# Weight sums by adding transfers that read DRAM, and six raw places as three pairs

## The chip, the cores and the metric

The kernel runs on one core of a Trainium2 chip. The metric is the device time of one execution in microseconds (us): the median of three runs before the change is 1502.31 us (1502.04 to 1503.32). A profile of one further execution shows what each engine did in it. The engines are TensorE (PE, with its weight loads PEld), VectorE (DVE), ScalarE (ACT), GpSimd (POOL) and SyncE (SP), and 16 DMA engines move data.

## The reference, cut to what matters

The layer normalises, mixes tokens in three branches, and then runs an MLP. The change lies in the MLP, on 256 tokens, with D_MODEL 2048 and D_FF 8192, all float32:

```python
x = x + _rms_norm(mix, norm_mix_post[l])
hdn = jnp.square(jax.nn.relu(_rms_norm(x, norm_mlp_pre[l]) @ w_mlp_up[l]))
x = x + _rms_norm(hdn @ w_mlp_down[l], norm_mlp_post[l])
```

## The kernel before

All big weights lie in DRAM as one stream `wst` of pieces of 128 x 1024 float32 (512 KB), in the order of use. A piece goes from DRAM to a raw tile by a DMA that SP issues (line 162 in `wraw`, three places under the tag "raw"), and is then split into two parts of type float32r for TensorE: ScalarE copies it to `whi` with rounding (line 173), and VectorE subtracts that from the raw tile to get the rest, `wlo` (line 175). Each matmul is then done with the high part and, over half the columns or as a third product, the low one.

The mixing part, up to some 830 us, and the last stretch, from some 1441 us, use this stream alone, with an order that is partly written out by hand (`manual_schedule`). Between them lies the stretch that the change touches. It interleaves two kinds of work:

- *up products* (`up`, lines 1370 to 1383): 64 hidden column blocks, each in two halves, each half with one piece of the up weights from the stream (`wraw`, line 162) and 16 matmuls in `gemm` (lines 191, 195, 197). `hidden` (lines 1348 to 1368) then makes the squared relu of the sum and `forms` (lines 1385 to 1397) the seven combinations of four parts of the hidden tensor that the next kind needs.
- *down products* (`down`, lines 1399 to 1475): for most of the hidden rows the product with `w_mlp_down` is done in Winograd's form of a two by two block product, with seven multiplications for eight. There are 28 blocks: four groups of 3, 4, 4 and 3 (`SIZES`) by two column halves `sb`. A block has four weight quarters, called "22", "12", "11" and "21", each 128 x 1024 in SBUF.

The seven products of a block need the quarters and running sums of them. `prep(f, d)` makes the operand of product `f` (line 1408). For f = 3 it loads 22 and 12 (`braw`, DMA at line 1331), splits 22, and VectorE adds 12 to 22 (line 1411). For f = 7 it loads 11, splits 22, VectorE adds 11 to 22, and a DMA that GpSimd issues adds 11 to 12 (`dma_add`, line 1414, with `accum_op` add, from tile to tile). For f = 1 it splits 11. For f = 6 it loads 21, splits 22, and a DMA adds 21 to 22. f = 2 splits 21, f = 5 splits 12 and f = 4 splits 22. `run(f, d, hl)` issues the six matmuls of a product (lines 1434 to 1436), and `post` adds finished sums to the output tiles (line 1441).

A block of the list (lines 1541 to 1554) is: product 3, an up half, product 4 of the block before, then products 7 and 1, an up half, 6 and 2, an up half, 5, an up half. The eight blocks in `THREE` (numbers 18, 20, 21 and 23 to 27, counted from 0) have three up halves instead of four. `drive` (line 1301) prepares an item one ahead of the item that runs. The order of instructions on each engine is not written out in this stretch: the framework's planner makes it from the order in the program and from its own costs, and it puts in the waits.

The raw tiles of the quarters share one tag, "raw2", with six places. A place is free for the next load once everything that reads or writes the tile in it is done: the splits, VectorE's sums, and the adding transfer that reads it as a source or writes it as a target. SP issues loads of both tags in one queue, so a load that waits for its place holds every load behind it.

A quarter in DRAM is two runs of 512 columns in each of 128 rows of two neighbouring pieces of the stream (`second` gives the number of the first), so a load by `braw` has 256 runs of 2 KB; a load at line 162 has 128 runs of 4 KB. The adding transfer before reads 128 rows of 4 KB of one tile and adds them to 128 rows of another.

At the end, the split parts of the last three pieces of the stream get places of their own from tag "raw2" (`spare`, line 1567).

Of the kernel before, what the change touches and what calls it, by code (L numbers as in the profile page):

```python
# [11 lines left out]
F32 = mybir.dt.float32  # L12
F32R = mybir.dt.float32r
AF = mybir.ActivationFunctionType
ALU = mybir.AluOpType
# [8 lines left out]
HALF = 1024  # L24
# [28 lines left out]
def hybrid_block(ctx, tc, xt, x, gains, params, consts, lora, gup, wst, out):  # L53
    nc = tc.nc
    V, A, G, PE = nc.vector, nc.scalar, nc.gpsimd, nc.tensor
# [10 lines left out]
    def nm(s):  # L66
        uid[0] += 1
        return f"{s}_{uid[0]}"

    def gps():  # L70
        return pg.tile([128, 512], F32, tag="gps", name=nm("gps"), bufs=4)

    def mps():
        return pm.tile([128, 512], F32, tag="mps", name=nm("mps"), bufs=4)
# [207 lines left out]
    def g1(w=T):  # L282
        return rp.tile([128, T], F32, tag="g1", name=nm("g1"), bufs=21)
# [772 lines left out]
    for hf in range(2):  # L1056
        for s, mo in (("k", MU_K), ("r", MU_R), ("v", MU_V)):
            for p in range(4 * hf, 4 * hf + 4):
                ps = unit(upk)
                d = g1()  # L1060
# [99 lines left out]
    for c in range(0, D, 512):  # L1160
        for tt in range(2):
            loads.append(lambda tt=tt, c=c: nc.sync.dma_start(out=x1[tt][:, c:c + 512],
                                                              in_=x[tt * 128:tt * 128 + 128, c:c + 512]))
# [3 lines left out]
    def junk():  # L1167
        return p2.tile([128, 512], F32, tag="junk", name=nm("junk"), bufs=2)
# [153 lines left out]
    def second(g, cg):  # L1322

        return base + 64 * (g // 4) + 32 + 8 * cg + 2 * (g % 4)

    def braw(c0, d, n):

        i, j = int(n[0]) - 1, int(n[1]) - 1
        u = second(d, c0 // 512 + j)
        raw = p3.tile([128, HALF], F32, tag="raw2", name=nm("raw"), bufs=6)  # L1330
        nc.sync.dma_start(out=raw.rearrange("p (r c) -> p r c", r=2),
                          in_=wst[u:u + 2, :, 512 * i:512 * i + 512].rearrange("r p c -> p r c"))
        return raw

    def parts(raw):
        wsplit(raw)
        return wq.pop()
# [61 lines left out]
    def down(q, sb):  # L1399

        d0 = sum(SIZES[:q])
        dn = d0 + SIZES[q] - 1
        Q, R, vx = {}, {}, {}
        c0 = 1024 * sb
        y11, y12 = ys[0][:, c0:c0 + 512], ys[0][:, c0 + 512:c0 + 1024]
        y21, y22 = ys[1][:, c0:c0 + 512], ys[1][:, c0 + 512:c0 + 1024]

        def prep(f, d):

            def add(a, b):  # L1410
                V.tensor_tensor(R[d, a], R[d, a], R[d, b], ALU.add)  # L1411

            def dma_add(a, b):
                G.dma_start(out=R[d, a], in_=R[d, b], accum_op=ALU.add)  # L1414

            for n in {3: ("22", "12"), 7: ("11",), 6: ("21",)}.get(f, ()):
                R[d, n] = braw(c0, d, n)
            r = parts(R[d, {1: "11", 2: "21", 5: "12"}.get(f, "22")])
            if f == 3:
                add("22", "12")  # L1420
            elif f == 7:
                add("22", "11")
                dma_add("12", "11")
            elif f == 6:
                dma_add("22", "21")
            return r

        def run(f, d, hl):
            if d == d0:
                Q[f] = gps() if f in (3, 7, 1) else mps()  # L1430
            for i in range(2):
                a, b = fmh[2 * d + i][:, AF_[f], :], fml[2 * d + i][:, AF_[f], :]
                w, wl = (x[:, 512 * i:512 * i + 512] for x in hl)
                PE.matmul(Q[f], a, w, start=d == d0 and i == 0, stop=False)  # L1434
                PE.matmul(Q[f], b, w, start=False, stop=False)  # L1435
                PE.matmul(Q[f], a, wl, start=False, stop=d == dn and i == 1)  # L1436
            if d == dn:
                post(f)

        def acc(y, p, op=ALU.add):  # L1440
            sums.append(lambda: V.tensor_tensor(y, y, p, op))

        def first(y, p, op=ALU.add):

            if q == 0:
                sums.append(lambda: A.activation(y, p, AF.Copy, scale=1.0 if op == ALU.add else -1.0))
            else:
                acc(y, p, op)

        def post(f):  # L1450

            if f == 3:
                first(y12, Q[3], ALU.subtract)
            elif f == 1:
                first(y11, Q[1])
            elif f == 6:
                v = vx["v"] = junk()
                posts.append(lambda: A.activation(v, Q[6], AF.Copy))
                acc(v, Q[1], ALU.subtract)
                acc(y12, v)  # L1460
                acc(v, Q[7], ALU.subtract)
                first(y22, v)
            elif f == 2:
                acc(y11, Q[2])
            elif f == 5:
                acc(y12, Q[5], ALU.subtract)
                acc(y22, Q[5], ALU.subtract)
            elif f == 4:
                first(y21, Q[4])
                acc(y21, vx["v"], ALU.subtract)  # L1470

        def item(f, d):
            return (lambda: prep(f, d), lambda hl: run(f, d, hl), 0)

        return [{f: item(f, d) for f in range(1, 8)} for d in range(d0, dn + 1)]

    po.close()
    p3 = ctx.enter_context(tc.tile_pool(name="p3", bufs=1))
# [88 lines left out]
    def spare(n):  # L1567

        if n < wst.shape[0] - 3:
            return None  # L1570
        return [p3.tile([128, HALF], F32, tag="raw2", name=nm("kw"), bufs=6).bitcast(F32R) for _ in range(2)]

    home[0] = spare
    for g in range(4):
        gs = slice(512 * g, 512 * g + 512)
        for tt, ps in enumerate(tok(hp, 4 if g == 3 else 1)):
# [8 lines left out]
            if g == 3:  # L1585
                for c, w in (0, 512), (512, 512), (1024, 512), (1536, 256), (1792, 256):
# [3 lines left out]
                        out=out[tt * 128:tt * 128 + 128, cs], in_=x1[tt][:, cs])  # L1590
# [125 lines left out]
```

## Time and profile before

| | |
|---|---|
| median of three runs | 1502.31 us |
| the profiled execution | 1503.08 us, its span 1501.2 us |
| DMA, whole span | 312.19 MB, mean 208 GB/s; from HBM 279.24 MB |
| adding transfers | 56, of 512 KB each |
| loads of quarters | 112, of 512 KB each |
| loads by line 162 | 398, of 512 KB each |

How to read the rows that follow: a time in front of a row of the timeline or of the chain of waits is its start in us from the start of the span. `raw<-in_wst_dram` is a load, `raw<-raw` an adding transfer, q1 the queue of SP's transfers and q0 that of GpSimd's. SPq is SP's queue. In a row of waits stand the total in us, the count and the longest. In a row of groups stand, behind the bar, the busy time, the mean of one in ns, and the idle time before them with what ended it. For a transfer, the last number of its row is the median us from issue to landing. The line numbers are those of the kernel before.

### The profile page before, as it was taken

The numbers are of one execution on the slowest core, as the hardware profiler recorded it, in microseconds if no ns is written. First come the engines' busy times: TensorE is split into PE (matmuls) and PEld (weight loads), VectorE is DVE, ScalarE is ACT, GpSimd is POOL, SyncE is SP. The second block draws the span as 40 slices with busy tenths as digits, with TensorE's granted clock in tenths as the row PEclk, the third lists the DMA queues.
The fourth block names the chain that finished last, engine by engine and source line by source line (L and its number), as shares of the span: only waits on it lengthen the run. The fifth ranks groups of instructions, "written<-read, shape, count | busy, mean of one in ns | idle before, by whom it ended". The sixth has DMA issues, their size and how long they took to land.

```text
span 1501.2 us, 22710 instructions
## 1 busy us (share of the span) xinstructions
PE 1487.4 (99%) x8384; PEld 1250.2 (83%) x8384; DVE 1205.8 (80%) x1677; ACT 933.3 (62%) x1431; POOL 94.7 (6%) x151
## 2 busy tenths in 40 slices
PE   9999999999999999999999999999999999999997
PEld 8888888887788887788888888888888888888886
DVE  7965779895687895476557688998999989999996
ACT  7665677555765445564545676776666666767663
POOL 0011003000002000000000000000000000000000
PEclk9999999999999999999999999999999999999999
DMA  8655445454555455455774868889898888989874
GB/s 288 202 154 175 154 161 172 152 182 154 164 174 174 156 183 183 131 174 191 243 235 153 267 181 256 250 223 260 259 257 256 229 268 250 262 259 262 255 218 148
DMA packets 107055, 312.19 MB, mean 208 GB/s; under 512 B 12352, under 2 KB 14400, under 8 KB 106944
## 3 DMA queue, kind: packets, MB, share of 16 engines
q1 hardware_dynamic: 96336, 279.35, 57.0%
q0 software_dynamic: 8064, 29.36, 10.3%
q10 hardware_dynamic: 2544, 2.03, 0.5%
q8 instruction: 66, 1.08, 0.3%
q14 instruction: 45, 0.37, 0.1%
HBM read 279.24 MB, written 2.10 MB: 187 GB/s over the span
## 4 chain that ended last, share of the span: by engine, by line
PE 96%; DMA 1%; DVE 1%; issue 1%; ACT 1%; SPq 0%; POOLq 0%; DVEq 0%; POOL 0%; ACTq 0%
PE gps L235 28%; PE gps L191 22%; PE gps L195 12%; PE gps L220 7%; PE mps L1434 3%; PE mps L1436 3%; PE mps L1435 3%; PE gps L1436 2%; PE gps L1434 2%; PE gps L1435 2%; PE gps L197 2%; PE gps L359 1%; DMA raw<-raw 1%; PE mps L840 1%; DMA raw<-in_wst_dram 1%
## 5 line engine op out<-in xcount | busy, mean ns | idle before, releaser
L175 DVE TENSOR_TENSOR wlo<-raw,whi 128x1024 fp32r<-128x1024 f32 x570 | 691.3, 1223 | 151.0 <-ACT whi L173 140.6
L173 ACT ACTIVATE whi<-raw 128x1024 fp32r<-128x1024 f32 x570 | 597.6, 1057 | 253.7 <-PE gps L235 71.8
L191 PE MATMUL gps<-pk,whi 128*128 128x512 f32 x1460 | 370.6, 392 | 0.5 <-DVE tmp L1352 0.2
L191 PEld LDWEIGHTS gps<-pk,whi 128*128 128x128 f32 x1460 | 270.4, 188 | 56.2 <-DVE tmp L1352 1.2
L235 PE MATMUL gps<-whi,pk 128*128 128x512 f32 x1004 | 253.5, 392 | 0.0
L195 PEld LDWEIGHTS gps<-pk,wlo 128*128 128x128 f32 x1561 | 212.7, 190 | 15.2 <-DVE wlo L175 0.3
L235 PEld LDWEIGHTS gps<-whi,pk 128*128 128x128 f32 x1004 | 186.5, 188 | 40.1 <-issue 1.0
L195 PE MATMUL gps<-pk,wlo 128*128 128x256 f32 x1561 | 218.0, 282 | 0.0
L235 PE MATMUL gps<-wlo,pk 128*128 128x512 f32 x502 | 138.2, 392 | 0.0
L235 PEld LDWEIGHTS gps<-wlo,pk 128*128 128x128 f32 x502 | 93.2, 188 | 19.6 <-issue 0.2
L1434 PE MATMUL mps<-whi,fm 128*128 128x512 f32 x224 | 88.6, 396 | 1.8 <-ACT whi L173 1.7
L1351 ACT ACTIVATE tmp<-gps 128x256 f32<-128x256 f32 x64 | 24.6, 385 | 102.8 <-PE gps L197 100.9
L1435 PE MATMUL mps<-whi,fm 128*128 128x512 f32 x224 | 87.7, 392 | 0.0
L1436 PE MATMUL mps<-wlo,fm 128*128 128x512 f32 x224 | 87.4, 390 | 0.0
L1414 POOL DMA_DIRECT2D raw<-raw x56 | 48.8, 872 | 572.7 <-DVE raw L1411 299.1
L1411 DVE TENSOR_TENSOR raw<-raw,raw 128x1024 f32<-128x1024 f32 x56 | 68.3, 1220 | 0.8
L1434 PE MATMUL gps<-whi,fm 128*128 128x512 f32 x168 | 65.8, 392 | 0.0
L1436 PE MATMUL gps<-wlo,fm 128*128 128x512 f32 x168 | 65.7, 391 | 0.0
L1435 PE MATMUL gps<-whi,fm 128*128 128x512 f32 x168 | 65.5, 390 | 0.0
L220 PE MATMUL gps<-whi,pk 128*128 128x512 f32 x224 | 60.7, 393 | 0.0
L1434 PEld LDWEIGHTS mps<-whi,fm 128*128 128x128 f32 x224 | 42.4, 189 | 10.0 <-ACT whi L173 3.9
L1436 PEld LDWEIGHTS mps<-wlo,fm 128*128 128x128 f32 x224 | 42.1, 188 | 9.4
(359 smaller groups left out, 1738.3 us busy)
## 6 DMA issues: line engine op xcount, KB each, us to landing
raw<-in_wst_dram SPq DMA_DIRECT2D x510, 512.0 KB, 4.4
raw<-raw POOLq DMA_DIRECT2D x56, 512.0 KB, 8.5
x<-in_xt_dram SPq DMA_DIRECT2D x8, 256.0 KB, 5.3
x<-in_x_dram SPq DMA_DIRECT2D x8, 256.0 KB, 5.3
raw<-in_wst_dram SPq DMA_DIRECT2D x6, 256.0 KB, 5.0
pk<-in_wst_dram SPq DMA_DIRECT2D x6, 256.0 KB, 5.2
g<-in_gains_dram SPq DMA_DIRECT2D x4, 256.0 KB, 4.8
pk<-in_gains_dram SPq DMA_DIRECT2D x4, 256.0 KB, 6.7
```

Source lines behind the costliest of these rows:

```text
L173: A.activation(hi, raw, AF.Copy)
L175: low = lambda: V.tensor_tensor(lo, raw, hi.bitcast(F32), ALU.subtract)
L191: PE.matmul(ps, hi[:, i * 128:i * 128 + 128], pks[i], start=first and i == 0, stop=False)
L195: PE.matmul(ps[:, 0:T], lo[:, i * 128:i * 128 + 128], pks[i][:, 0:T], start=False, stop=False)
L197: PE.matmul(ps, hi[:, (n - 1) * 128:n * 128], pks[n - 1], start=False, stop=True)
L220: PE.matmul(ps[tt], pks[k][:, c:c + 128], w[:, (k - k0) * 512:(k - k0) * 512 + 512], start=k == 0 and part == 0 and w is hl[0], stop=w is ...
L235: PE.matmul(ps[tt], pks[k][:, c:c + 128], w[:, (k - k0) * 512:(k - k0) * 512 + 512], start=k == 0 and part == 0 and w is hl[0], stop=False)
L1411: V.tensor_tensor(R[d, a], R[d, a], R[d, b], ALU.add)
L1414: G.dma_start(out=R[d, a], in_=R[d, b], accum_op=ALU.add)
L1434: PE.matmul(Q[f], a, w, start=d == d0 and i == 0, stop=False)
L1435: PE.matmul(Q[f], b, w, start=False, stop=False)
L1436: PE.matmul(Q[f], a, wl, start=False, stop=d == dn and i == 1)
```

## The change

The adding transfer reads the quarter from DRAM again instead of from the tile that was loaded from it. The view of a quarter in DRAM becomes a function of its own, `block`, that the load and the adding transfer share. The one tag with six places becomes three tags with two places each: one for 22, one for 12, one for 11 and 21. The six tiles of the last three pieces take two from each tag. The loads of 11 and 21 stay, since products 1 and 2 and one of VectorE's sums use them.

```diff
-    def braw(c0, d, n):
+    def block(c0, d, n):
 
         i, j = int(n[0]) - 1, int(n[1]) - 1
         u = second(d, c0 // 512 + j)
-        raw = p3.tile([128, HALF], F32, tag="raw2", name=nm("raw"), bufs=6)
-        nc.sync.dma_start(out=raw.rearrange("p (r c) -> p r c", r=2),
-                          in_=wst[u:u + 2, :, 512 * i:512 * i + 512].rearrange("r p c -> p r c"))
+        return wst[u:u + 2, :, 512 * i:512 * i + 512].rearrange("r p c -> p r c")
+
+    def braw(c0, d, n):
+
+        raw = p3.tile([128, HALF], F32, tag={"22": "r22", "12": "r12"}.get(n, "r1"), name=nm("raw"), bufs=2)
+        nc.sync.dma_start(out=raw.rearrange("p (r c) -> p r c", r=2), in_=block(c0, d, n))
         return raw
...
             def dma_add(a, b):
-                G.dma_start(out=R[d, a], in_=R[d, b], accum_op=ALU.add)
+                G.dma_start(out=R[d, a].rearrange("p (r c) -> p r c", r=2), in_=block(c0, d, b), accum_op=ALU.add)
...
-        return [p3.tile([128, HALF], F32, tag="raw2", name=nm("kw"), bufs=6).bitcast(F32R) for _ in range(2)]
+        tag = ("r22", "r12", "r1")[n - wst.shape[0] + 3]
+        return [p3.tile([128, HALF], F32, tag=tag, name=nm("kw"), bufs=2).bitcast(F32R) for _ in range(2)]
```

## The prediction

> **What bounds the kernel now.** I read the page's busy times first, then a table of stages, then the waits, and the chain of waits last.
>
> ```profile
> span 1501.2 us, 22710 instructions
> ...
> PE 1487.4 (99%) x8384; PEld 1250.2 (83%) x8384; DVE 1205.8 (80%) x1677; ACT 933.3 (62%) x1431; POOL 94.7 (6%) x151
> ...
> DMA  8655445454555455455774868889898888989874
> ```
>
> TensorE (PE) is busy 99% of the span, so nothing that shortens another engine's work helps unless PE waits for it. The DMA row is the second thing to see: from about 880 us on, the stage that the change touches, the 16 DMA engines are busy eight or nine tenths of the time. The same stage in windows (busy us of five engines, granted clock, DMA share, GB/s):
>
> ```profile
> core 0: us, PE busy (x) PEld busy (x) DVE busy (x) ACT busy (x) POOL busy (x), PEclk, DMA share, GB/s
> 880.00:960.00 80.00, 80.00 (x413) 68.33 (x412) 71.82 (x85) 55.96 (x80) 7.07 (x8) 1.00 0.82 236
> ...
> 1040.00:1120.00 80.00, 79.91 (x408) 68.00 (x407) 71.95 (x80) 53.98 (x73) 6.53 (x8) 1.00 0.88 251
> 1120.00:1200.00 80.00, 78.72 (x402) 66.70 (x401) 75.34 (x94) 54.67 (x77) 6.96 (x8) 1.00 0.86 244
> 1200.00:1280.00 80.00, 79.73 (x406) 67.56 (x405) 72.99 (x83) 52.19 (x68) 6.96 (x8) 1.00 0.89 258
> 1280.00:1360.00 80.00, 79.92 (x406) 67.48 (x406) 77.97 (x96) 56.28 (x78) 6.96 (x8) 1.00 0.89 262
> 1360.00:1441.00 81.00, 80.33 (x400) 67.41 (x399) 76.41 (x82) 56.84 (x76) 7.83 (x9) 1.00 0.91 250
> ```
>
> PE's idle time here adds up to 0.09 + 1.28 + 0.27 + 0.08 + 0.67 = 2.4 us. Ends of matmuls are modelled, so the period of the blocks is the better measure. The chain has one eight-matmul row at the same place of each block with four up halves:
>
> ```profile
> 906.04 1.81 PE gps L191 x8
> ...
> 1071.59 1.81 PE gps L191 x8
> 1073.40 0.95 PE gps L195 x8
> ...
> 1091.10 10.11 DMA raw<-raw
> 1101.82 8.44 DMA raw<-in_wst_dram
> 1113.07 2.14 PE gps L191 x8
> ...
> 1260.10 1.81 PE gps L191 x8
> ```
>
> Eight blocks from 906.04 to 1071.59 give 20.69 us each. The next nine, to 1260.10, took 188.51 us where nine undisturbed ones take 186.24: PE lost 2.3 us. There the windows above show an idle of 0.09 + 1.28 = 1.37, so the period shows 1.7 times what the idle does. By the same factor the 1.02 us idle after 1200 is some 1.7 us. The ceiling of any gain in this stage is thus about 4.0 us.
>
> What did PE wait for? The chain says it for the first place: an adding transfer (10.11 us) held a load, the load landed 8.44 us later, and PE came out of it at 1113.07. For the second place the timeline says it:
>
> ```profile
> 1184.35 0.87 POOL L1414 DMA_DIRECT2D raw<-raw  x1 [9.21 <-DMA raw<-in_wst_dram]
> 1184.58 0.38 SPq L1331 DMA_DIRECT2D raw<-in_wst_dram  x1
> ...
> 1185.05 0.42 SPq L162 DMA_DIRECT2D raw<-in_wst_dram  x1
> ...
> 1193.67 0.37 SPq L1331 DMA_DIRECT2D raw<-in_wst_dram  x1
> ...
> 1194.34 1.06 ACT L173 ACTIVATE whi<-raw 128x1024 fp32r<-128x1024 f32 x1 [3.59 <-DMA raw<-in_wst_dram]
> ...
> 1197.19 0.50 PE L1434 MATMUL mps<-whi,fm 128*128 128x512 f32 x1 [1.04 <-ACT whi L173]
> ...
> 1198.17 2.14 PE L191 MATMUL gps<-pk,whi 128*128 128x512 f32 x8 [0.24 <-DVE tmp L1352]
> ...
> 1201.08 0.40 PE L1436 MATMUL mps<-wlo,fm 128*128 128x512 f32 x1
> ```
>
> The adding transfer issued at 1184.35 is in flight until SP's next load can go at 1193.67; ACT meanwhile sits 3.59 us for a load, and PE after it. The waits of SP's queue in this stage, and POOL's (us in total, times, longest):
>
> ```profile
> SPq L1331 <- DMA raw<-raw: 310.6, 54, 9.3
> SPq L162 <- DVE wlo L175: 78.6, 46, 6.0
> SPq L1331 <- DVE wlo L175: 46.1, 33, 2.7
> ...
> POOL raw L1414 <- DMA raw<-in_wst_dram: 56.4, 6, 11.1
> ...
> ACT whi L173 <- DMA raw<-raw: 0.9, 1, 0.9
> ```
>
> SP stood 310.6 of 560 us behind adding transfers, because the six raw places were held by a source or a target of one, and every load behind in the queue, those of the up weights (L162) too, stood with it. Yet of the 54 waits PE felt two: the buffers cover the rest.
>
> **The change part by part.** *Removed waits of SP.* The source tile of an adding transfer is no longer read by it, so 11 is free after its split for product 1 and the sum with 22, and 21 after product 2. With a pair per kind, 22 and 12 of a block take the place of two blocks before, last used by products 4 and 5 of that block; 11 and 21 take the place that 11 and 21 of the block before left. When prep issues a load, all of these lie most of a block (20.69 us) back. So the 54 waits go, and the 33 on DVE at the same line. What SP waits for next is L162's 46 waits for the three up places, 78.6 us in all, 1.7 us each, which delayed nothing so far.
>
> *Removed wait of POOL.* The add no longer needs the landing of its source (6 waits, 56.4 us); it still needs that of its target and the VectorE work on it (299.1 us of its idle time in the row further below). Nothing else of this stage stands on POOL. So an add can go earlier, never later.
>
> *The transfer itself.* This is the unknown. Queues in two windows, the first 700 us and then 880 to 1440:
>
> ```profile
> q1 hardware_dynamic: 36784, 120.73, 53.7%
> ...
> q1 hardware_dynamic: 43952, 110.11, 59.5%
> q0 software_dynamic: 8000, 29.17, 27.3%
> ```
>
> ```profile
> raw<-in_wst_dram SPq DMA_DIRECT2D x510, 512.0 KB, 4.4
> raw<-raw POOLq DMA_DIRECT2D x56, 512.0 KB, 8.5
> ...
> L175 DVE TENSOR_TENSOR wlo<-raw,whi 128x1024 fp32r<-128x1024 f32 x570 | 691.3, 1223 | 151.0 <-ACT whi L173 140.6
> ...
> L1414 POOL DMA_DIRECT2D raw<-raw x56 | 48.8, 872 | 572.7 <-DVE raw L1411 299.1
> ```
>
> A load: 59.5% of 16 x 560 us is 5331 us for 110.11 MB, 48.4 us a MB, 1.59 us on all 16 engines for 512 KB (0.524 MB). In the first 700 us, with larger packets (3.3 against 2.5 KB), it is 49.8 us a MB: halving a packet shows no price. An add: 27.3% is 2446 us for 29.17 MB, 83.9 us a MB, 2.75 us each, or 0.306 us for each of 8000 packets.
>
> After, each add reads 128 x 2 runs of 512 numbers from DRAM instead of 128 rows of 1024. Bounds: if the DRAM read runs beside the read of the target, an add costs as little as a load, 1.59 us; if its price is by the packet, with 272 (256 and 16 small ones) for 144, 272 x 0.306 / 16 = 5.2 us. I take the load's price for the source and half the add's for the target, 48.4 + 42 = 90.4 us a MB, 2.96 us, because the one thing that these rows price twice goes by bytes. That is 0.21 x 56 = 12 us more engine time: the DMA share goes from 59.5 + 27.3 = 86.8% to 88.9%.
>
> The Trainium skill has a rule against the change (DMA: Bandwidth & Descriptors, "Why small descriptors are slow (HBM only)"): each packet has a fixed overhead of about 3 cycles beside 32-byte beats, and SBUF to SBUF is spared the penalty of small ones that HBM has. By it 2 KB packets cost (64 + 3) / 64 against (128 + 3) / 128, an estimate of 2.3% or 0.06 us an add, which would leave the sum where it is; the two q1 rows show not even that.
>
> POOL writes the descriptors in 872 ns; for twice as many, between 0.87 and 1.65 us, hidden in its 572.7 us of idle. With the 0.21 us an add then lands at most 1.0 us later than its 8.5 us median. What covers it: from product 7, which starts the add on 12, to product 5, which uses it, lie four products and two up halves. An up half is 1.81 + 0.95 = 2.76 us (the rows at 1071.59 and 1073.40); a block of 20.69 us with four of them leaves 9.65 for seven products, 1.38 each; together 11.0 us. In blocks with three up halves one up half less lies between, 8.3 us, less than the landing, and there the earlier issue has to pay for the later end. Today's adds nearly always suffice (one wait of ACT, 0.9 us).
>
> *DRAM traffic* grows by the 29.4 MB of the adds, some 52 GB/s over the stage. The two loads of 11 and 21 stay. *The last three weights* take their homes from the three pairs:
>
> ```profile
> 1475.53 1.06 ACT L173 ACTIVATE kw<-raw 128x1024 fp32r<-128x1024 f32 x1
> ```
>
> That is 34 us after the stage's last window ends at 1441, when all three pairs are long free: nothing.
>
> **Sum.** Against the profiled execution (1503.08 us, span 1501.2 and 1.9 outside): the 2.3 us of the two places behind adding transfers go. The 1.7 us after 1200 have another owner for most of it: VectorE is busy 77.97 of 80 us there. I credit a quarter, 0.4. Sum -2.7: 1500.4 on that execution, which lies 0.8 above the median of the runs, so 1499.6.
>
> **Rivals.**
>
> A, the forecast: gain 1.3 to 4.0 us, 1498.3 to 1501.0.
>
> B, hidden anyway: SP's waits go, but the lost time comes back at VectorE, 90 to 97% busy in the stage. For it: only 2 of 54 waits reached PE. Against: both of these are seen to start with an adding transfer. 1501.0 to 1503.
>
> C, slower by order: the order of this stage isn't written out, a planner makes it from its own times, and already interrupts a product (L1436 at 1201.08 stands behind an up product begun at 1198.17). With loads early in its reckoning it may put a product where the split is not done. One such place costs PE a split on ACT and one on VectorE, 1.06 + 1.22 = 2.3 us. It decides from three places (6.9 less the 2.7 gained: +4.2, 1506.5); at one in each of eight half quarters +15.7, 1518. For it: the early add removes two constraints at once. Against: eight blocks in a row run at 20.69 without a loss.
>
> D, slower by DMA: adds nearer to 5.2 us. The last stretch decides:
>
> ```profile
> q1 hardware_dynamic: 14960, 36.70, 58.3%
> q0 software_dynamic: 2821, 10.30, 30.9%
> ```
>
> From 1255 to 1440 these fill 89.2%; 20.0 us are free for 2821 / 144 = 19.6 adds, so the engines are full from 2.92 + 1.02 = 3.9 us an add. Over the stage, 560 us less 5331 / 16 gives each of 55.6 adds 4.1. At 5.2 the adds and the loads need 289 + 333 = 622 us for 560: +62, 1564. For it: a software queue that has only read SBUF so far, and DMA at nine tenths. Against: prices by bytes. The Trainium skill (same page, "Latency and other measured facts") gives an HBM access as 0.2 us on average and 2 us at high load; if an add waited out 0.2 us for each of its 16 packets an engine, an estimate of 3.2 us on top, D would hold. No row here shows an add that reads DRAM.
>
> **How the numbers follow.** 0.2% (3.0 us), about what a measurement of this kernel can tell from no change, puts the bounds at 1499.3 and 1505.3. A has 0.52, with 0.28 of it below 1499.3 as the loss after 1200 may go too; B 0.12; C 0.16; D 0.20. Faster 0.28; same 0.24 + 0.12 = 0.36; slower 0.36. A's own range is 1498.3 to 1501.0. The range for 8 in 10 must take in C's usual part and D's beginning: 1498.0 to 1512, with most of D and C's end left out, under 0.2.
>
> **What would show it.** Right: no SP wait on an adding transfer, POOL's wait for loads gone; 20.69 us blocks from 906 to 1260 without the 2.3; software queue share near 29%, some 15,200 packets; VectorE still near 78 of 80 after 1280. Wrong: a share of that queue above 38% (D), PE idle behind ACT or VectorE where no load is late (C), or adds that land after 13 us and hold product 5.

## The result and the profile after

| | median | ratio to before, 95% interval |
|---|---|---|
| before | 1503.51 us (21 runs) | |
| changed | 1505.45 us (21 runs) | 1.0017, 1.0011 to 1.0023 |

The change makes the kernel slower, by 1.9 us between the medians and by 2.6 us after the ratio, where the prediction had it faster by 2.7. The page of the changed kernel, in the rows that answer to those of before:

```profile
span 1503.7 us, 22659 instructions
...
PE 1488.8 (99%) x8384; PEld 1251.4 (83%) x8384; DVE 1206.2 (80%) x1677; ACT 933.6 (62%) x1431; POOL 113.3 (8%) x151
...
DMA  8645455454555455455674769989989998998964
...
L1417 POOL DMA_DIRECT2D raw<-in_wst_dram x56 | 67.5, 1205 | 554.2 <-DVE raw L1414 279.4
...
raw<-in_wst_dram POOLq DMA_DIRECT2D x56, 512.0 KB, 8.7
```

At this level little is to be seen: an add's descriptors take POOL 1205 ns instead of 872, and an add lands in a median of 8.7 us instead of 8.5. (Lines are three higher than before: the adds stand at 1417, VectorE's sums at 1414, the loads of quarters at 1335.) The waits of SP in the stage, again total, times and longest:

```profile
SPq L162 <- DVE wlo L175: 194.7, 89, 6.9
SPq L1335 <- DVE wlo L175: 144.1, 76, 6.2
```

The 54 waits on adding transfers, 310.6 us, are gone. SP still waits, but for splits on VectorE, and more often than before: 89 and 76 times in these two rows, where it was 46 and 33. In the first two thirds of the stage PE's time went as the prediction said. In windows (PE, PEld, DVE, ACT, POOL busy; clock; DMA share; GB/s), first of before, then of the changed kernel:

```profile
880.00:1255.00 375.00, 373.63 (x1914) 318.70 (x1913) 342.76 (x400) 258.16 (x355) 31.41 (x36) 1.00 0.86 247
1255.00:1360.00 105.00, 104.64 (x528) 87.91 (x527) 101.87 (x121) 71.39 (x97) 9.56 (x11) 1.00 0.89 258
1360.00:1441.00 81.00, 80.33 (x400) 67.41 (x399) 76.41 (x82) 56.84 (x76) 7.83 (x9) 1.00 0.91 250
1441.00:1460.00 19.00, 19.00 (x89) 15.87 (x88) 17.26 (x23) 10.05 (x15) 0.00 (x0) 1.00 0.71 232
```

```profile
880.00:1255.00 375.00, 374.96 (x1923) 320.59 (x1923) 344.70 (x403) 258.73 (x357) 43.43 (x36) 1.00 0.91 250
1255.00:1360.00 105.00, 104.64 (x528) 87.95 (x527) 101.92 (x121) 72.25 (x97) 13.23 (x11) 1.00 0.89 247
1360.00:1441.00 81.00, 79.15 (x392) 66.04 (x391) 74.96 (x80) 55.62 (x75) 10.83 (x9) 1.00 0.90 249
1441.00:1460.00 19.00, 17.60 (x83) 14.22 (x82) 14.80 (x20) 8.46 (x12) 0.00 (x0) 1.00 0.65 194
```

To 1255 us PE's idle time falls from 1.37 to 0.04 us. After 1360 it rises from 0.67 to 1.85, and after 1441, where before had none, to 1.40. What stands there is shown by the chain of waits of the changed kernel:

```profile
1382.80 9.86 DMA raw<-in_wst_dram
1392.77 1.07 ACT whi L173
...
1437.73 9.00 DMA raw<-in_wst_dram
1446.84 1.07 ACT whi L173
```

Both DMA rows are second adds of a block, 21 to 22, issued after the split for product 6 and needed by the split for product 4. The second is the very last add of the kernel. No up product is left behind it, so ACT stands from the end of its earlier work until the landing, and PE behind ACT. The timeline at that place, before and changed:

```profile
1436.89 0.87 POOL L1414 DMA_DIRECT2D raw<-raw  x1 [7.42 <-DVE wlo L175]
...
1437.77 0.33 SPq L162 DMA_DIRECT2D raw<-in_wst_dram  x1
...
1442.86 2.01 ACT L173 ACTIVATE whi<-raw 128x1024 fp32r<-128x1024 f32 x2 [1.66 <-DMA raw<-raw]
```

```profile
1437.73 1.20 POOL L1417 DMA_DIRECT2D raw<-in_wst_dram  x1 [7.42 <-DVE wlo L175]
...
1438.28 0.33 SPq L162 DMA_DIRECT2D raw<-in_wst_dram  x1
1438.65 0.91 SPq L1140 DMA_DIRECT2D pk<-in_gains_dram  x2
...
1446.84 2.01 ACT L173 ACTIVATE whi<-raw 128x1024 fp32r<-128x1024 f32 x2 [5.13 <-DMA raw<-in_wst_dram]
...
1447.95 0.50 PE L1437 MATMUL mps<-whi,fm 128*128 128x512 f32 x1 [0.88 <-ACT whi L173]
...
1449.21 0.50 PE L1439 MATMUL mps<-wlo,fm 128*128 128x512 f32 x1 [0.53 <-DVE wlo L175]
```

Before, ACT waited 1.66 us for this add, and PE still had work; after the change it waited 5.13 us, because the add landed 9.0 us after its issue instead of 5.9.

The median over all adds hides this, as there are two kinds. From the issue and landing of each of the 56 adds in the trace (the first and the second of each block, means of 28): the first lands in 9.1 us before and 8.2 after, the second in 7.3 before (7.7 in blocks 4 to 26) and 8.9 after. Adding up, for each second add of blocks 4 to 26, the time that other transfers, nearly all of them SP's, held the 16 engines during its flight gives 3.9 us before and 4.9 after.

The order of the instructions on TensorE, VectorE and ScalarE is the same in both kernels, row for row. SP issues its transfers in the same order too; what differs is when it issues them, and what POOL's adds read. With PE's extra starts over the usual interval between matmuls as the measure, PE loses 1.9 us less up to 1260 us, then 1.5 more after 1360 and 1.9 more after 1441: +1.5 us. The rest of the 2.5 us between the two spans, 1.0, arises in the first 346 us, where the two programs don't differ, and in other profiles of the study the part ahead of the stage differs from that of before by -0.2 to 1.2 us. So the trace accounts for 1.5 us of the slowdown. Of the kernel before there is one profile, so whether its two stalls come in every execution isn't shown. One execution of the study, the profiled one of the first run with the last add on VectorE, was a slow one of 5254.79 us, and that run's ratio leaves it out.

### The profile page after: what moved, and what is told of

It is laid out like the page before. It is cut to its first block, busy times and chain, and to the rows that moved or that the text cites. A ratio compares the mean times of both kernels' runs of the same rounds, so it can differ in the third digit from the quotient of the medians.

```text
span 1503.7 us, 22659 instructions
## 1 busy us (share of the span) xinstructions
PE 1488.8 (99%) x8384; PEld 1251.4 (83%) x8384; DVE 1206.2 (80%) x1677; ACT 933.6 (62%) x1431; POOL 113.3 (8%) x151
## 3 DMA queue, kind: packets, MB, share of 16 engines
q0 software_dynamic: 15232, 29.36, 12.2%
## 4 chain that ended last, share of the span: by engine, by line
PE 92%; issue 3%; DMA 2%; DVE 2%; ACT 1%; POOL 0%; SPq 0%; POOLq 0%; DVEq 0%; ACTq 0%
PE gps L235 27%; PE gps L191 22%; PE gps L195 12%; PE gps L220 7%; PE mps L1437 3%; PE mps L1439 3%; PE mps L1438 3%; PE gps L1439 2%; PE gps L1437 2%; PE gps L1438 2%; DMA raw<-in_wst_dram 2%; PE gps L197 1%; DVE wlo L175 1%; PE gps L359 1%; PE mps L840 1%
## 5 line engine op out<-in xcount | busy, mean ns | idle before, releaser
L1417 POOL DMA_DIRECT2D raw<-in_wst_dram x56 | 67.5, 1205 | 554.2 <-DVE raw L1414 279.4
```

Of the source, the lines that this page charges most:

```text
L1417: G.dma_start(out=R[d, a].rearrange("p (r c) -> p r c", r=2), in_=block(c0, d, b), accum_op=ALU.add)
```

## The experiments

Two theories stood at first. Theory Q: SP's waits on adds had held loads back, and so had given the second add the engines to itself. Rival P: an add that reads DRAM costs more by itself. All edits below are against the changed kernel. Times are medians in us, of 11 executions each (1 KB runs: 4), and ratios are to runs of before on the same chip. "First" and "second" are the mean landing times of the two adds of a block, worked out as above, and "held" is the time of the other transfers during the second add.

| kernel | time | ratio, 95% interval | first | second | held |
|---|---|---|---|---|---|
| changed, again | 1505.27 | 1.0012 (1.0003 to 1.0021) | 8.2 | 9.0 | 4.9 |
| pairs only, adds from tiles | 1502.06 | 0.9996 (0.9987 to 1.0005) | 7.5 | 5.9 | 2.4 |
| DRAM adds, six places | 1505.36 | 1.0015 (1.0006 to 1.0024) | 8.1 | 9.0 | 4.8 |
| gains later | 1503.93 | 1.0005 (0.9996 to 1.0014) | 8.2 | 9.0 | 5.0 |
| last add on VectorE | 1502.73 | 0.9999 (0.9990 to 1.0007) | | | |
| 4 KB runs, loads and adds | 1501.78 | 0.9993 (0.9984 to 1.0002) | 6.3 | 7.0 | 2.9 |
| 4 KB runs, adds alone | 1501.42 | 0.9990 (0.9981 to 1.0000) | 6.9 | 7.3 | 3.6 |
| 4 KB runs, loads alone | 1504.65 | 1.0011 (1.0002 to 1.0019) | 8.1 | 8.8 | 4.6 |
| 1 KB runs, adds alone | 1520.16 | 1.0110 (1.0095 to 1.0125) | 8.8 | 10.4 | 6.2 |
| tile adds, 4 KB loads | 1502.23 | 0.9995 (0.9986 to 1.0004) | 7.1 | 5.9 | 2.3 |
| 4 KB runs, product 4 later | 1500.97 | 0.9987 (0.9978 to 0.9996) | 6.6 | 7.9 | 4.5 |

**The halves of the change.** First the three pairs without the DRAM source:

```diff
-                G.dma_start(out=R[d, a].rearrange("p (r c) -> p r c", r=2), in_=block(c0, d, b), accum_op=ALU.add)
+                G.dma_start(out=R[d, a], in_=R[d, b], accum_op=ALU.add)
```

> Three pairs of places, but the adds read tiles as before. Theory Q (queue): SP's waits on adds held loads back while an add was in flight, and so gave the second add of a block (21 to 22) the DMA engines; with the waits gone loads stand ahead of it. Then the waits on adds shrink from 310 us to under 100, the second add lands in a mean of 8.3 us or more (7.7 before, 8.9 after the change), and PE loses about as much after 1360 us as in the changed kernel (1.5 us or more). Rival P (price): the DRAM add itself is what costs, 1.2 us of descriptors for 0.87 and 3.3 us of engines for 2.7. Then this kernel has the second add back at 7.7 us and the time is that of before or up to 2 us less.

Then the DRAM source without the pairs:

```diff
-        raw = p3.tile([128, HALF], F32, tag={"22": "r22", "12": "r12"}.get(n, "r1"), name=nm("raw"), bufs=2)
+        raw = p3.tile([128, HALF], F32, tag="raw2", name=nm("raw"), bufs=6)
...
-        tag = ("r22", "r12", "r1")[n - wst.shape[0] + 3]
-        return [p3.tile([128, HALF], F32, tag=tag, name=nm("kw"), bufs=2).bitcast(F32R) for _ in range(2)]
+        return [p3.tile([128, HALF], F32, tag="raw2", name=nm("kw"), bufs=6).bitcast(F32R) for _ in range(2)]
```

> The adds read DRAM, but the six places stay one tag. Theory P: descriptors 1.2 us, engines 3.3 us an add as in the changed kernel, so its time too, 1504.5 to 1506.5, and the last add lands in 9 us. Theory Q: the result follows the waits of SP that are left: with over 150 us of them behind places, the second add has a mean of 8.3 us or less and the time is nearer to before; with few, it is the changed kernel's.

SP's waits, of the pairs alone and then of the DRAM source alone:

```profile
SPq L1335 <- DMA raw<-raw: 235.0, 53, 8.0
SPq L162 <- DVE wlo L175: 133.3, 61, 5.9
```

```profile
SPq L162 <- DVE wlo L175: 193.8, 89, 7.0
SPq L1335 <- DVE wlo L175: 143.5, 76, 6.2
```

With the source in DRAM the waits on adds vanish whatever the places are, and the waits are those of the whole change; with the pairs alone 53 of them stay. So the DRAM source alone does both what was wanted and the harm, and the pairs add nothing to it. Theory Q had foreseen that the pairs free SP; they don't, and so the first of its tests is void: with 235 us of waits left, the second add is quicker than before (5.9 us), PE's two stalls at 1113 and 1197 us are gone, and there is none at the end. The gain of 1.9 us thus comes with most of SP's waits on adds still there, and which of them had caused the two stalls stays open. Rival P, which had forecast both times, stands up to here.

**What the last add is late for.** The four loads of gains, of which two land within 1.8 us after the last add's issue and two are issued within 1.4 us after it, were put behind weight loads:

```diff
-    side.extend(loads)
+    def behind_load(f):
+        with tc.issue_after(rawdma[0].ins):
+            f()
+
+    side.extend([lambda f=f: behind_load(f) for f in loads])
```

> As the changed kernel, but the four 256 KB loads of gains at the end go one behind each of the next four weight loads instead of ahead of them. Nothing about the adds changes. Theory Q: the last add has 1.6 us less of loads ahead of it, lands in 7.5 us or less instead of 9.0, and PE's loss of 1.9 us at 1447 to 1449 us falls to under 0.7; the time falls by 1 to 1.5 us. Theory P: the last add stays at 9 us and the loss stays.

The queues and the issue of the last add between 1436 and 1448 us, changed kernel and then with the gains later (the last number is the median from issue to landing):

```profile
q1 hardware_dynamic: 837, 2.04, 54.9%
...
raw<-in_wst_dram POOLq DMA_DIRECT2D x1, 512.0 KB, 9.0
```

```profile
q1 hardware_dynamic: 433, 1.31, 41.4%
...
raw<-in_wst_dram POOLq DMA_DIRECT2D x1, 512.0 KB, 7.3
```

With 1.31 instead of 2.04 MB of SP's transfers beside it, the same add lands 1.7 us earlier. PE's loss after 1441 us falls from 1.9 to 0.2 us and the median by 1.5 us. Here theory Q's core, that loads beside the add delay it, holds, and P alone falls: nothing of the add itself was changed.

The packets of this add in the trace show what else delays it. Before the change, its packets began 1.5 us after its issue, and those of the weight load that SP issued 0.88 us after it (1437.77 against 1436.89) only at 4.35 us. In the changed kernel the load is issued 0.55 us after the add (1438.28 against 1437.73): PE's progress taken as the measure, the add comes 0.34 us later and the load at the same time, and POOL's instruction takes 0.33 us longer. There the load's packets begin at 1.5 us, and the add's at 3.8. Moving the gains leaves that as it is (1.5 and 3.8 us); it shortens what follows. So the last add has lost its place ahead of a whole load.

The same place from the other side: the very last add on VectorE.

```diff
-                dma_add("22", "21")
+                (add if q == 3 and sb == 1 and d == dn else dma_add)("22", "21")
```

> As the changed kernel, but the very last add (21 to 22 in block 27) is done by VectorE from the loaded tile, 1.22 us. Both theories put PE's loss of 1.9 us at 1447 to 1449 us on that add landing late, so it goes to under 0.3 and the time falls by 1.3 to 1.9 us. Were the end stall due to the loads of the last stretch instead, it would stay.

> As the changed kernel, with the very last add done by VectorE from the loaded tile. PE's loss of 1.9 us at 1447 to 1449 us goes to under 0.3, the rest stays as in the changed kernel; 1503 to 1504.

The first of these two runs gave 1503.54 us (ratio 1.0000, 0.9991 to 1.0009). In the second the loss after 1441 us is 0 and the time 1502.73, 2.5 us below the changed kernel on the same chip; somewhat more than the 1.9 us of that place, though the two intervals overlap.

**The length of the runs.** The host can lay the two pieces of a pair out so that a quarter is one piece of 128 rows of 4 KB:

```diff
-        return wst[u:u + 2, :, 512 * i:512 * i + 512].rearrange("r p c -> p r c")
+        return wst[u + i]
...
-                G.dma_start(out=R[d, a].rearrange("p (r c) -> p r c", r=2), in_=block(c0, d, b), accum_op=ALU.add)
+                G.dma_start(out=R[d, a], in_=block(c0, d, b), accum_op=ALU.add)
...
+    base = len(o) - 256
+    for g in range(14):
+        for cg in range(4):
+            u = base + 64 * (g // 4) + 32 + 8 * cg + 2 * (g % 4)
+            o[u], o[u + 1] = [np.concatenate([o[u][:, c:c + 512], o[u + 1][:, c:c + 512]], 1) for c in (0, 512)]
     return np.stack(o)
```

> As the changed kernel, but a quarter lies in DRAM as 128 runs of 4 KB (the two pieces of each pair are rearranged on the host), so loads and adds have half the packets. Theory P: descriptors come back to 0.87 us and an add to 2.7 us on the engines; the second add falls by about 0.9 us to 8.0 and the losses after 1360 us go, 1502 to 1503.5. Theory Q: loads still stand ahead of the second add; it falls by no more than the 0.9 us of its own and the blocks with three up halves still lose over 1 us.

It did better than either theory had forecast: the second add falls by 1.9 us, twice the 0.9 that both had put down to its own price, PE's idle time after 1360 us is that of before (0.67 us), and the time is some 3.6 us below the changed kernel's. SP is as free as in the changed kernel. So Q in its first form, freed loads alone, isn't the cause either; short runs without freed loads were not run. This led to theory T: with packets half as long, the adds let more of the loads past.

To see whether the runs of the loads or those of the adds matter, a second copy of the quarters in this layout was put beside the stream (`wqt`), and only one of the two reads it. The order of the instructions on all five engines is then that of the changed kernel.

```diff
+    def whole_block(c0, d, n):
+
+        return wqt[8 * d + 2 * (c0 // 512 + int(n[1]) - 1) + int(n[0]) - 1]
...
-                G.dma_start(out=R[d, a].rearrange("p (r c) -> p r c", r=2), in_=block(c0, d, b), accum_op=ALU.add)
+                G.dma_start(out=R[d, a], in_=whole_block(c0, d, b), accum_op=ALU.add)
```

> As the changed kernel, but the adds read a second copy of the quarters in DRAM, laid out as 128 runs of 4 KB; the loads keep their 2 KB runs. The order on every engine is that of the changed kernel. Theory T (turns): the DMA engines serve the queues in turns of one packet, so an add of 16 packets an engine lets twice as many load packets past as one of 8. Then the second add falls from a mean of 8.9 us to 7.5 or less, load time during its flight from 4.9 to under 3.5, the end stall of 1.9 us goes, and the time falls by 2 to 3.5 us to that of before or below. Rival L (loads): it was the loads of 4 KB that sped up the kernel with long runs; the second add stays above 8.3 us and the time at 1504.5 or more.

```diff
-        nc.sync.dma_start(out=raw.rearrange("p (r c) -> p r c", r=2), in_=block(c0, d, n))
+        nc.sync.dma_start(out=raw, in_=whole_block(c0, d, n))
```

> The other half: the loads of the quarters read the copy with 4 KB runs, the adds keep their 2 KB runs; order as in the changed kernel. Theory T: nothing gained, the second add at 8.5 us or more, the end stall of 1.5 us or more stays, 1504.5 to 1506.5. Rival L: the second add at 7.5 us or less and the time 1502 to 1503.

And the adds in the other direction, with a copy that holds a quarter as 512 runs of 1 KB:

```diff
-        return wqt[8 * d + 2 * (c0 // 512 + int(n[1]) - 1) + int(n[0]) - 1]
+        v, i = 4 * (4 * d + c0 // 512 + int(n[1]) - 1), 256 * (int(n[0]) - 1)
+        return wqt[v:v + 4, :, i:i + 256].rearrange("r p c -> p r c")
```

> As the changed kernel, but the adds read a copy of the quarters in DRAM as 512 runs of 1 KB; loads and the order on every engine stay. Theory T (turns of one packet): 32 packets an engine let still more load packets past, so the load time during the second add's flight rises from 4.9 to over 5.5 us, it lands in a mean of 10 us or more, and the time is 1508 or more. Rival P (own price alone): only the descriptors grow, by about 0.7 us, so 9.6 us at most with unchanged load time, and 1505.5 to 1507.5.

Three kernels, then, that differ in the length of the adds' runs, and the middle one also in reading the stream itself instead of a copy. For each, POOL's row (behind the bar: busy, mean ns of one), the adds' queue in the stage from 880 to 1440 us, and who waited for the adds (us in all, times). Adds in 4 KB runs:

```profile
L1421 POOL DMA_DIRECT2D raw<-in_wqt_dram x56 | 49.0, 875 | 570.6 <-DVE raw L1418 288.3
...
q0 software_dynamic: 8046, 29.36, 31.4%
...
  ACT whi L173: 1.6, 1
```

Adds in 2 KB runs, the changed kernel:

```profile
q0 software_dynamic: 14960, 28.84, 32.3%
...
  ACT whi L173: 10.6, 6
```

Adds in 1 KB runs:

```profile
L1422 POOL DMA_DIRECT2D raw<-in_wqt_dram x56 | 72.0, 1286 | 565.8 <-DVE raw L1419 270.5
...
q0 software_dynamic: 28245, 28.06, 32.9%
...
  ACT whi L173: 35.2, 21
```

The engine time of an add hardly moves: 31.4% of 16 x 560 us for 29.36 MB is 95.8 us a MB, 3.14 us an add; by the same way 3.29 and 3.44. POOL's descriptors take 875, 1205 and 1286 ns. But the second add lands in 7.3, 8.9 and 10.4 us, the other transfers hold the engines for 3.6, 4.9 and 6.2 us of its flight, and ACT waits for adds 1, 6 and 21 times (4 in the second profile of the changed kernel, 2 before the change). From 2 to 1 KB the add's own parts grow by 0.08 + 0.15 = 0.2 us, and the landing by 1.5, of which 1.3 are the loads. That decides against P, an add's own price alone: more load time passes during an add of shorter runs. The loads' runs alone give nothing (8.8 us, 1504.65).

It doesn't show theory T's turns of one packet. Counting an add as begun when one in twenty of its packets has started, the second adds of blocks 4 to 26 begin in a mean of 1.9, 3.2 and 3.9 us after their issue with 4, 2 and 1 KB runs, and land 5.3, 5.6 and 6.4 us after that. So of the 1.6 us that the changed kernel loses to 4 KB runs, 1.3 lie ahead of the add's own packets, and turns among these packets can have made only the rest. With 4 KB runs every one of these adds begins between 1.6 and 2.7 us; with 2 KB runs they begin between 2.1 and 5.1, which leaves room for a whole load ahead, as with the last add. The last add with 4 KB runs is in front of its load again: it begins at 1.6 us, the load at 4.4.

**Whether the DRAM source is worth anything.** Pairs, adds from tiles, and the loads in the long layout (the two diffs of pairs only and long runs together):

> Three pairs, adds from tiles, and loads in 4 KB runs. It tells whether the DRAM source is worth anything once runs are long. Theory T: adds of 8 packets an engine with SP held during part of them, so the second add at 6 us or less, no end stall, 1501 to 1502.5, no faster than the kernel with DRAM adds of long runs (1501.78), since PE's other losses are not due to adds. If the DRAM source brings a gain of its own by freeing SP, this one is slower by over 1 us.

1502.23 us against 1501.78 and 1501.42, intervals that overlap widely. In its profile PE waits 2.0 us for the low part of an up weight at 1358 us, after ACT had stood 2.42 us for a load at 1353. The two kernels with DRAM adds in 4 KB runs don't show that wait; whether SP's remaining waits on adds (227.9 us) caused it isn't shown, and one execution doesn't settle it.

**A better version.** With long runs, product 4 of the block before moved behind products 7 and 1:

```diff
-            work.extend([F[3], *some(1), *last])
+            work.extend([F[3], *some(1)])
...
-                work.extend([*form(need), F[7], F[1], *some(1), F[6], F[2], *some(1), *form(need), F[5], *some(1)])
+                work.extend([*form(need), F[7], F[1], *last, *some(1), F[6], F[2], *some(1), *form(need), F[5], *some(1)])
...
-                work.extend([F[7], F[1], F[6], *some(1), *form(need), F[2], F[5], *some(1), *form(need)])
+                work.extend([F[7], F[1], *last, F[6], *some(1), *form(need), F[2], F[5], *some(1), *form(need)])
```

> Long runs for loads and adds, and product 4 of the block before moved behind products 7 and 1, 2.8 us later. If adds still set something there, PE's remaining 2.4 us in this stage shrink and the time is 1 us or more below the kernel with long runs (1501.78). If VectorE and ScalarE set them, nothing changes or a new order costs 1 to 3 us.

1500.97 us: 0.8 below long runs alone, less than the 1 us asked for and with intervals that overlap, and the only kernel whose interval lies wholly below before. The order of the instructions differs here, and the second add lands later again (7.9 us), so that the adds were what still cost time isn't shown. Between 1255 and 1441 us PE idles 0.14 us here:

```profile
1255.00:1360.00 105.00, 104.92 (x530) 88.62 (x529) 101.66 (x121) 72.80 (x98) 9.59 (x11) 1.00 0.86 250
1360.00:1441.00 81.00, 80.94 (x402) 67.69 (x402) 76.97 (x84) 55.51 (x75) 7.86 (x9) 1.00 0.89 254
```

Finally the changed kernel once more:

> The changed kernel once more, on the chip of the others: 1504.5 to 1506.5, with PE's losses again after 1380 us and at 1447 to 1449 us if they belong to the kernel and not to one execution.

1505.27 us, and PE's idle time in its second profile is 2.07 us from 1360 to 1441 and 1.71 from 1441 to 1460: the losses belong to the kernel.

## Why the prediction was wrong

*Removed waits of SP: right, for half the reason given.* The 54 waits on adds went, and most of the 2.3 us in the blocks up to 1260 with them. But the DRAM source alone removes the waits, since then no add holds 11 or 21; the pairs alone leave 53, and there the 1.9 us are gained all the same. The 33 waits on VectorE at the same line didn't go with them: they became 76.

*"An add can go earlier, never later": hardly any did.* With PE's progress as the measure, every add is issued within 0.4 us of its time before, the last one 0.34 us later, as an add still waits for VectorE's work on its target. So the earlier issue that had to pay for the later end in blocks with three up halves never came.

*The price of the transfer: the term was nearly right.* 2.96 us and 29% of the queue were forecast; 3.29 us and 32.3% came. Descriptors at 1.2 us lay within 0.87 to 1.65, though no row gives that upper bound. An add's price stayed below the 3.9 us at which rival D would have filled the engines, and D didn't happen.

*The landing and its cover: the step that failed.* The prediction let an add land "at most 1.0 us later than its 8.5 us median", adding only the add's own time, and set that against the cover of the first add, from product 7 to product 5. Three things were wrong in it. The median mixed two kinds (9.1 and 7.3). What grew wasn't the add's own time but the load time that passes during its flight: with runs half as long the second add lands 1.6 us later, of which only 0.3 us are descriptors and 0.15 engine time, and most of the rest lies ahead of its first packets. And the cover that was thin was the second add's, from product 6 to product 4, thinnest behind the last block, where no up product is left. For the add issued at 1382.80 ACT stood ready after 7.9 us (a landing of 9.86 less a wait of 1.95), for the last one after 3.9 (9.00 less 5.13). The "one wait of ACT, 0.9 us" was already one for a second add, and the last add's wait of 1.66 us before the change, at 1442.86, lay just behind the window that the prediction had read. "Halving a packet shows no price" was read from engine time per byte, which is true of engine time alone, and from packets of 2.5 against 3.3 KB, which isn't half.

*The credit after 1200 us.* 0.4 us were credited there; PE lost 1.5 us more after 1360 and 1.9 after 1441. The gain of 1.9 us and these losses are the net of the trace.

*The rivals.* C (order) is out: the orders of the three engines are the same. B (hidden anyway) is out: the trace has the gain where it was placed. The forecast's last sentence named late adds, but at 13 us and for product 5; they came at 9 to 10 us and for product 4.

*The rule on small descriptors.* The Trainium skill ("Why small descriptors are slow (HBM only)" in DMA: Bandwidth & Descriptors) had given an estimate of 0.06 us an add; from 4 to 2 KB the engines took 0.15 us more. The same page says under "Queues, rings and completion order" that each DMA engine takes its queues in turn and drains a packet of some 9 to 17 descriptors before it switches. By it an add of 8 runs an engine would pass in one turn and one of 16 in one or two, an estimate. The last add with 4 KB runs agrees as far as it can be seen: from 1.6 to 4.4 us after its issue, none of the packets of the load behind it began, which turns of a single run would not give. But the trace doesn't tell one engine's packets from another's, so the turns themselves aren't shown. Nor is why the second adds begin 1.3 us later with 2 KB runs than with 4 KB, when the descriptors differ by only 0.3.

## What to carry to other kernels

The engine time of a transfer and its landing are two prices: here, beside a busy queue, an add cut into shorter runs took nearly the same engine time and landed later, while more of the other queue's work passed it. So look for the transfers that something waits for, take their landings by kind and not as one median, and find the one with the thinnest cover, here the last, which has no work behind it. Look there too at which transfer's packets begin first. Where a transfer must be quick beside others, try long runs, by the layout in DRAM if need be.

## What was not expected of the hardware

An adding transfer's engine time changes by a quarter at most with its source and its runs: 2.75 us for 512 KB from a tile, 3.14 from DRAM in 4 KB runs, 3.29 in 2 KB and 3.44 in 1 KB. The mean landing of the second adds ranges from 5.9 us to 10.4 in the same stage.

The time that POOL's instruction takes grows far less than the number of runs that it describes: 875 ns for 128 runs, 1205 for 256 and 1286 for 512.
